# Unsplit tokens from DMAs that add, an earlier pair of gate blocks, and a later due time for the output weights

## The chip, the cores and the metric

The kernel runs on one core of a Trainium2 chip. Its time is the device time of that core in microseconds (us), lower is better. One core has five engines, each with an instruction stream of its own that is executed in order: TensorE (PE, matmuls, with its weight loads shown as PEld), VectorE (DVE), ScalarE (ACT), GpSimd (POOL) and SyncE (SP, which here does nothing but issue DMAs). They meet only through semaphores. DMAs move data beside them.

## The reference

One hybrid layer over 16 meta tokens and 512 tokens, model width 1024. The same RMS-normalised input feeds softmax attention of 8 heads and a gated delta recurrence of 8 heads; each is gated, projected, weighed with a sigmoid, added, projected again and added to the input.

```
hn = rms_norm(h, norm_w)
proj = hn @ w_in
aq, ak, av, az, dq, dk, dv, dz, db, da, ga, gd = split(proj)
o_a = rms_norm(diff_attention(q, k, v, lam), attn_norm_w) * (1 - lam_init)
y_a = (o_a * silu(az)) @ w_branch_attn
qkv = silu(causal_depthwise_conv([dq, dk, dv], conv_w))
o_d = rms_norm(gated_delta_chunked(q, k, v, beta, g), dn_norm_w)
y_d = (o_d * silu(dz)) @ w_branch_delta
merged = sigmoid(ga) * y_a + sigmoid(gd) * y_d
out = rms_norm(h + merged @ w_out, final_norm_w)[:, N_META:]
```

## The kernel before

All of it stays on the chip, in float32 accuracy: each factor of a matmul is split into a high part in a 32-bit format that PE reads in one pass and a low part, what is left (tiles that end in `H` and `L`, or `wh` and `wl`), and three products, high by high, high by low and low by high, are added in PSUM (`PASSES`).

The work is a list of weight blocks of 128 columns (`ORDER`, made by `dense_order`). For each of four groups g there are two heads: keys `dk`, values `dv`, queries `dq` and gates `dz` of the delta rule, and `ak`, `av`, `aq`, `az` of attention. A weight block is fetched by SP into one of four `raw` buffers; ACT rounds it to `wh` and DVE forms `wl` (`load_weights`, `split`). Then PE multiplies it with the tokens `hnH`, `hnL`. Where two blocks come as a pair (`ak` with `av`, and `dk`, `dv` from the second group on) the kernel uses a seven-product scheme in place of eight (`pair_of_blocks`), which needs sums of the tokens too, not only the tokens.

Start: the input comes in as four blocks of 128 tokens `xt` and the 16 meta tokens `mt`. `normalise` takes the squares on ACT, the root on POOL (`rs`), the diagonal `dg` on DVE, and PE transposes and scales at once into a PSUM bank. Out of the bank, `part` writes `hnH` on ACT and `hnL` on DVE. Before the change a third reader, `whole` (L563 to L575), copies the unsplit value from the bank on ACT to the four buffers `room0` to `room3`, one for each half of the channels and each half of the tokens (`whole_`). The bank is free for the next block once both the copy and `hnL` are done. From the `room` buffers `token_sums` (L607) makes four differences on DVE, splits each (`sumH` on ACT, `sumL` on DVE) and so the pairs' sums. It waits for all copies and for the event `ap`, which comes at the end of `gates`, the decays of the delta rule. When the sums are done, `room0`, `room2` and `room3` become buffers for the gated outputs and for the gates `dz`, `az`: a gate block cannot leave its PSUM bank earlier.

End: two branch projections `yd` and `ya` in the same seven-product scheme (`pair_products`), in which ACT takes snapshots `sn` of a running PSUM bank, then the output projection, whose weights `wout` come as eight blocks through the same four `raw` buffers.

The instructions of all engines are put in order when the program is built: a planner (`Plan`) plays the work as tasks with ranks, a cost for each instruction (`Engine.time`), a landing time for each DMA (`transfer`, and `late`, which adds to it) and counts of free buffers, and the order in which an engine is reached is the order of its stream. On the chip each stream is then run in that order, and an instruction that waits holds up all behind it on its engine.

Almost every operation is recorded on one line of a helper (L231), so the profile's groups are told apart by their tiles.

Of the kernel before, what the change touches and what calls it, by code (L numbers as in the profile page):

```python
# [10 lines left out]
F32 = mybir.dt.float32  # L11
# [3 lines left out]
ALU = mybir.AluOpType  # L15
# [5 lines left out]
KB = D // P  # L21
# [12 lines left out]
def dense_order():  # L34

    order = []
    for g in range(H // 2):
        k, v, q, z = ([(n, 2 * g), (n, 2 * g + 1)] for n in ("dk", "dv", "dq", "dz"))
        a0, a1 = ([(n, 2 * g + i) for n in ("ak", "av", "aq", "az")] for i in range(2))
        order += k + v + (a0 + q + z[:1] if g else q + z[:1] + a0) + a1 + z[1:]  # L40
    order += [("gd", c) for c in range(KB)] + [("ga", 0)]
    for n in range(KB):
        order += [("ga", n + 1)] * (n < KB - 1) + [(("yd", "ya")[n // 4], 2 * (n % 4) + i) for i in range(2)]
    return order
# [17 lines left out]
HALF = L // 2  # L62
# [6 lines left out]
PE, DVE, ACT, POOL, SP = "PE", "DVE", "ACT", "POOL", "SP"  # L69
# [19 lines left out]
class Plan:  # L89
# [24 lines left out]
    def spawn(self, gen, rank=None):  # L114
        time, src = self.here() if self.task else (0.0, SP)
        self.tasks.append(Task(gen, self.task.rank if rank is None else rank, time, src))

    def done(self, event):
        self.events[event] = self.here()
# [96 lines left out]
class Engine:  # L216
# [18 lines left out]
    def time(self, op, args, kw):  # L235
        if op == "dma_start":
            return {SP: 60, ACT: 700, POOL: 1050}[self.name]
        out = kw["out"] if "out" in kw else args[0]
        ins = [a for a in list(args[1:]) + list(kw.values()) if hasattr(a, "dtype") and hasattr(a, "space")]
        n = int(np.prod(out.shape[1:]))  # L240
        if self.name == PE:
            if op == "transpose":
                return 2 * max(n / 2.4, 53)
            dt = ins[-1].dtype
            if dt == F32:
                small = ins[0].shape[0] <= 64
                return 2 * max(2 * n / 2.4 + 4, 32 if small else 107)
            if dt == F32R:
                return n / 2.4 + (11 if n < 400 else 18) if n >= 256 else max(2 * n / 2.4, 107)
            return n / 2.4 + 57  # L250
        psum = any(a.space == PSUM for a in ins)
        if op == "tensor_reduce":
            n = int(np.prod(ins[-1].shape[1:]))
        scalar = any(hasattr(kw.get(k), "space") for k in ("scalar", "scalar1", "scale", "bias"))
        if self.name == ACT:
            return (51 if op == "copy" and psum else 94) + n / 1.2 + 50 * scalar + 93 * ("accum_out" in kw)
        if self.name == DVE:
            one = op in ("tensor_copy", "tensor_scalar", "tensor_scalar_mul", "tensor_scalar_add", "memset")
# [7 lines left out]
def hybrid_block(ctx: ExitStack, tc: tile.TileContext, x, meta, wblk, wbd, wout, pcol, prow, out):  # L266
    nc = tc.nc
    plan = Plan({**SLOTS, "wo": 0, "th": 0}, BANKS, ALL_BANKS)
# [32 lines left out]
    def give(kind, at=None):  # L301
        plan.give(kind, names_.index(at.tensor.name) if kind in BANKS else 0)
# [9 lines left out]
    def tick(event, n):  # L312
        ticks[event] = ticks.get(event, 0) + 1
        if ticks[event] == n:
            done(event)
        return ticks[event] == n
# [159 lines left out]
    def load_weights(n):  # L476
        yield ("raw",)
        which = plan.task.slot
        raw = raws[which]
        yield SP  # L480
        m = n - len(ORDER)
        S.dma_start(out=raw, in_=wblk[n] if m < 0 else wout[m // 4, :, m % 4 * D:m % 4 * D + D])
        if n in PAIRED or m < 0 and ORDER[n][0] in ("yd", "ya"):
            first.append((raw, which))
            if len(first) == 2:
                spawn(split_pair(n - 1, tuple(first)), 0)
                first.clear()
        else:
            spawn(split(n, raw, which), 0.3 if n < 2 else 0 if m < 0 else 2)
# [34 lines left out]
    def normalise(n):  # L524

        yield f"x{n}"
        w = P if n == 0 else D
        ss, rs, dg = (mk(sp, [P, k], F32, t, 3) for k, t in ((1, "ss"), (1, "rs"), (P, "dg")))
        yield ACT
        A.activation(out=st[:, :w], in_=xt[n], func=AF.Square, accum_out=ss)  # L530

        def weigh():
            yield "nwb"
            yield DVE
            V.tensor_tensor(out=xt[n], in0=xt[n], in1=mt[:, P:2 * P] if n == 0 else nwb, op=ALU.mult)
# [12 lines left out]
        V.tensor_scalar(out=ss, in0=src, scalar1=1.0 / D, scalar2=EPS, op0=ALU.mult, op1=ALU.add)  # L548
        if n == 0:
            give("pdl", pt)  # L550
        yield POOL
        G.tensor_tensor(out=rs, in0=ss, in1=mhalf[:, 0:1], op=ALU.pow)
        yield DVE
        V.tensor_scalar_mul(out=dg, in0=ident, scalar1=rs)
        yield f"xw{n}"

        def part(pt, dst):
            yield ACT
            A.copy(out=hn[0][dst], in_=pt)
            tick(f"hh{n}", 1 if n == 0 else 2)  # L560
            bank_ = f"hn bank {n} {dst[1].start}"

            def whole():  # L563

                t0, t1 = dst[2].start, dst[2].stop
                for c in (0, KB // 2) if n == 0 else (dst[1].start,):
                    for m in range(2):
                        lo, hi = max(t0, HALF * m), min(t1, HALF * m + HALF)
                        if lo < hi:
                            yield ACT  # L570
                            A.copy(out=whole_[2 * (c // 4) + m][:, :, lo - HALF * m:hi - HALF * m],
                                   in_=pt[:, c - dst[1].start:c - dst[1].start + 4, lo - t0:hi - t0])
                if tick(bank_, 2):
                    give("pat", pt)
                tick("whole", 9)  # L575

            spawn(whole(), 0.6)
            yield DVE
            V.tensor_tensor(out=hn[1][dst], in0=pt, in1=hn[0][dst].bitcast(F32), op=ALU.subtract)
            if tick(bank_, 2):  # L580
                give("pat", pt)
            tick(f"hn{n}", 1 if n == 0 else 2)

        for hf in range(1 if n == 0 else 2):
            yield ("pat",)
            yield PE
            pt = bank("pat")
            if n == 0:
                T.matmul(pt[:, 0:P], xt[0], dg, start=True, stop=True)
                pt = pt[:, 0:P].rearrange("p (k t) -> p k t", t=NM)  # L590
                dst = (slice(None), slice(0, KB), slice(0, NM))
            else:
                pt = pt.rearrange("p (k t) -> p k t", t=P)
                for k in range(4):
                    T.matmul(pt[:, k, :], xt[n][:, (4 * hf + k) * P:(4 * hf + k + 1) * P], dg, start=True, stop=True)
                dst = (slice(None), slice(4 * hf, 4 * hf + 4), slice(NM + P * (n - 1), NM + P * n))
            spawn(part(pt, dst))
# [6 lines left out]
    ts_l = [mk(rp, [P, KB // 2, HALF], F32R, f"sumL{n}") for n in range(4)]  # L604
    of_sum = dict(t1=0, t2=3, t3=1, t4=2)

    def token_sums():  # L607
        yield "whole"
        yield "ap"

        def high_low(key):
            n = of_sum[key]
            yield ACT
            A.copy(out=ts_h[n], in_=whole_[n])
            yield DVE
            V.tensor_tensor(out=ts_l[n], in0=whole_[n], in1=ts_h[n].bitcast(F32), op=ALU.subtract)
            done(key)
            if tick("sums", 4):
                for n in range(SLOTS["th"]):
                    plan.give("th", n)  # L620

        for key, (x_, y_) in dict(t1=(1, 0), t3=(3, 1), t2=(3, 0), t4=(2, 3)).items():
            yield DVE
            V.tensor_tensor(out=whole_[of_sum[key]], in0=whole_[x_], in1=whole_[y_], op=ALU.subtract)
            spawn(high_low(key))
# [1579 lines left out]
```

## Time and profile before

| what | value |
|---|---|
| time, median of 3 runs | 765.07 us (760.48 to 768.07) |
| profiled execution | 767.75 us, span 766.0 us |
| granted TensorE clock, mean | 0.989 |
| instructions | 14381 |
| HBM read, written | 67.58 MB, 6.36 MB |

The span is what the trace shows from the first to the last instruction; the profiled execution's own time is 1.75 us longer. Each engine's row gives its busy time and count. A matmul's duration includes its way through the array, so that dense matmuls overlap in the trace: their cost is the distance between two starts. In a row of the timeline stand the start, the duration, the engine, the operation with output and inputs, the count, and, in brackets, the idle time ahead of it and who ended it.

### The profile page before, as it was taken

To read this page: it belongs to the slowest core of one execution; us is meant where nothing else is said; L and a number is where in the kernel's file an instruction comes from. 1 tells how busy PE (TensorE), PEld (TensorE's weight loads), DVE (VectorE), ACT (ScalarE), POOL (GpSimd) and SP (SyncE) were. 2 spreads that over 40 slices of the span, in tenths; PEclk is the share of its full clock that TensorE was granted. 3 is DMA by queue.
4 is the path that set the end of the run, shared out by engine and by line. 5 is a ranking of instruction groups with operands and counts; after the bars stand their busy time and mean duration, and the time that the engine had idled before them with its cause. 6 is when DMAs were issued, how large, how long until landed. Compare 5 with 4: busy or idle time off the path is not lost.

```text
span 766.0 us, 14381 instructions
## 1 busy us (share of the span) xinstructions
PE 740.0 (97%) x5311; PEld 671.6 (88%) x5311; DVE 620.2 (81%) x1427; ACT 500.4 (65%) x1318; POOL 89.6 (12%) x102
## 2 busy tenths in 40 slices
PE   4999999999999999999999999999999999999996
PEld 4998888899999799999889989988888998898775
DVE  6799999699899659989877979975697879797353
ACT  6479576679865848986587977667776446454132
POOL 4134002112000201401020311000100000000001
PEclk9999999999999979999999999999999999999999
DMA  8031423224304103421320441360123442143502
GB/s 320 30 113 32 135 83 70 70 70 149 98 33 145 31 34 119 147 81 42 118 64 22 159 135 33 120 184 30 56 83 116 147 148 91 57 131 111 193 1 110
DMA packets 45430, 74.86 MB, mean 98 GB/s; under 512 B 20728, under 2 KB 25636, under 8 KB 45360
## 3 DMA queue, kind: packets, MB, share of 16 engines
q1 hardware_dynamic: 45360, 73.95, 30.0%
q8 instruction: 41, 0.67, 0.3%
q14 instruction: 29, 0.24, 0.1%
HBM read 67.58 MB, written 6.36 MB: 97 GB/s over the span
## 4 chain that ended last, share of the span: by engine, by line
PE 74%; DVE 10%; ACT 10%; issue 2%; DMA 1%; POOL 1%; SPq 0%; POOLq 0%; DVEq 0%; ACTq 0%
PE bank L231 71%; PE psc L231 3%; ACT wh L231 2%; DVE wl L231 2%; DVE y L231 1%; ACT TM L231 1%; DMA xt<-in_x_dram 1%; POOL km L231 1%; ACT ak L231 1%; ACT e L231 1%; DMA raw<-in_wout_dram 1%; ACT ktd L231 1%; DVE ak L231 1%; DVE ast L231 1%; ACT y L231 1%
## 5 line engine op out<-in xcount | busy, mean ns | idle before, releaser
L231 PE MATMUL bank<-hnH,wh 128*128 128x512 f32 (+4 forms) x664 | 233.6, 355 | 1.6 <-ACT hnH L231 1.3
L231 PE MATMUL bank<-hnL,wh 128*128 128x512 f32 (+4 forms) x664 | 222.0, 337 | 0.0
L231 PE MATMUL bank<-hnH,wl 128*128 128x512 f32 (+4 forms) x664 | 221.7, 337 | 0.0
L231 DVE TENSOR_TENSOR wl<-raw,wh 128x1024 fp32r<-128x1024 f32 (+1 forms) x120 | 134.4, 1121 | 20.2 <-ACT wh L231 19.6
L231 ACT CAST wh<-raw 128x1024 fp32r<-128x1024 f32 (+1 forms) x120 | 116.4, 970 | 48.6 <-PE bank L231 34.5
L231 PEld LDWEIGHTS bank<-hnH,wh 128*128 128x128 f32 x664 | 124.5, 189 | 14.5 <-ACT hnH L231 1.5
L231 PEld LDWEIGHTS bank<-hnH,wl 128*128 128x128 f32 x664 | 124.3, 189 | 14.0
L231 PEld LDWEIGHTS bank<-hnL,wh 128*128 128x128 f32 x664 | 124.5, 189 | 9.5
L231 PE MATMUL bank<-sumH,wh 128*128 128x264 f32 x224 | 68.0, 303 | 0.0
L231 PE MATMUL bank<-sumL,wh 128*128 128x264 f32 x224 | 63.9, 285 | 0.4 <-DVE sumL L231 0.4
L231 PE MATMUL bank<-sumH,wl 128*128 128x264 f32 x224 | 63.8, 285 | 0.0
L231 DVE SCALAR_TENSOR_TENSOR y<-xp,pc,y 128x528 f32<-128x528 f32 (+1 forms) x72 | 54.1, 757 | 0.5 <-ACT y L231 0.5
L231 ACT ACTIVATE e<-psc,ast 128x144 f32<-128x144 f32 (+3 forms) x64 | 34.7, 542 | 18.4 <-DVE ast L231 16.6
L231 PEld LDWEIGHTS bank<-sumL,wh 128*128 128x128 f32 x224 | 42.6, 190 | 0.6 <-DVE sumL L231 0.6
L231 PEld LDWEIGHTS bank<-sumH,wh 128*128 128x128 f32 x224 | 42.7, 190 | 0.2
L231 PEld LDWEIGHTS bank<-sumH,wl 128*128 128x128 f32 x224 | 42.4, 189 | 0.0
L231 PE MATMUL bank<-btH,wh 128*128 128x256 f32 x128 | 36.2, 283 | 2.1 <-ACT sn L231 2.1
L231 PE MATMUL bank<-btH,wl 128*128 128x256 f32 x128 | 36.0, 281 | 0.0
L231 PE MATMUL bank<-btL,wh 128*128 128x256 f32 x128 | 35.9, 281 | 0.0
L231 POOL TENSOR_TENSOR ass<-ass,mhalf 128x4 f32<-128x4 f32 x8 | 10.3, 1288 | 186.8 <-DVE ass L231 175.2
L231 PE MATMUL psc<-ak,aq 128*128 128x264 f32 (+3 forms) x160 | 29.1, 303 | 0.4 <-ACT e L231 0.3
L231 DVE TENSOR_REDUCE ast<-psc 128x1 f32<-128x528 f32 (+3 forms) x40 | 28.5, 714 | 0.5
(370 smaller groups left out, 1738.2 us busy)
## 6 DMA issues: line engine op xcount, KB each, us to landing
raw<-in_wblk_dram SPq DMA_DIRECT2D x96, 512.0 KB, 3.6
raw<-in_wout_dram SPq DMA_DIRECT2D x8, 512.0 KB, 4.9
xt<-in_x_dram SPq DMA_DIRECT2D x4, 512.0 KB, 6.4
TM<-gcd SPq DMA_DIRECT2D x8, 256.0 KB, 5.9
xr<-in_x_dram SPq DMA_DIRECT2D x8, 256.0 KB, 6.0
out_dram<-xr SPq DMA_DIRECT2D x8, 256.0 KB, 2.1
room<-scrm SPq DMA_DIRECT2D x12, 128.0 KB, 3.5
oad<-room SPq DMA_DIRECT2D x6, 256.0 KB, 2.0
```

Of the source, the lines that this page charges most:

```text
L231: return real(*args, **kw)
```

## The change

Three edits.

1. `whole` no longer copies on ACT out of PSUM. It is a task for each of the four `room` buffers: SP issues a DMA that copies `hnH` (528 KB of it) into the buffer, and when that has landed POOL issues two DMAs, each of which adds half of the `hnL` part to it in flight. `token_sums` waits for all four. In `part` a bank is given back once `hnL` is formed.
2. In the first group the order is now `dk`, `dv`, `dq`, both `dz`, then the four blocks of the first attention head and those of the second; the second `dz` block stood behind the heads before. In the other groups nothing moves.
3. The planner is told that blocks of `wout` land 1600 ns later than it reckoned, and that a small float32 matmul costs 40 ns.

```
-        order += k + v + (a0 + q + z[:1] if g else q + z[:1] + a0) + a1 + z[1:]
+        order += k + v + (a0 + q + z[:1] + a1 + z[1:] if g else q + z + a0 + a1)
...
-                return 2 * max(2 * n / 2.4 + 4, 32 if small else 107)
+                return 2 * max(2 * n / 2.4 + 4, 32 if small else 107) if n > 32 or ins[0].shape[0] > 32 else 40
...
         S.dma_start(out=raw, in_=wblk[n] if m < 0 else wout[m // 4, :, m % 4 * D:m % 4 * D + D])
+        if m >= 0:
+            plan.late(1600)
...
             tick(f"hh{n}", 1 if n == 0 else 2)
-            bank_ = f"hn bank {n} {dst[1].start}"
-
-            def whole():
...
-                            A.copy(out=whole_[2 * (c // 4) + m][:, :, lo - HALF * m:hi - HALF * m],
-                                   in_=pt[:, c - dst[1].start:c - dst[1].start + 4, lo - t0:hi - t0])
-                if tick(bank_, 2):
-                    give("pat", pt)
-                tick("whole", 9)
-
-            spawn(whole(), 0.6)
             yield DVE
             V.tensor_tensor(out=hn[1][dst], in0=pt, in1=hn[0][dst].bitcast(F32), op=ALU.subtract)
-            if tick(bank_, 2):
-                give("pat", pt)
+            give("pat", pt)
...
+    def whole(c, m):
+
+        part = slice(None), slice(KB // 2 * c, KB // 2 * c + KB // 2), slice(HALF * m, HALF * m + HALF)
+        for e in range(1 if m == 0 else 2, 4 if m == 0 else 5):
+            yield f"hh{e}"
+        yield "hh0"
+        yield SP
+        S.dma_start(out=whole_[2 * c + m], in_=hn[0][part].bitcast(F32))
+        plan.late(1500)
+        for e in range(1 if m == 0 else 2, 4 if m == 0 else 5):
+            yield f"hn{e}"
+        yield "hn0"
+        low = hn[1][part].bitcast(F32)
+        for k in (0, 2):
+            yield POOL
+            G.dma_start(out=whole_[2 * c + m][:, k:k + 2], in_=low[:, k:k + 2], accum_op=ALU.add)
+        plan.late(5000)
+        done(f"whole {c}{m}")
+
     def token_sums():
-        yield "whole"
+        for c in range(2):
+            for m in range(2):
+                spawn(whole(c, m))
+        for c in range(2):
+            for m in range(2):
+                yield f"whole {c}{m}"
         yield "ap"
```

Three places show what moves in the streams. The first is ACT at the start, where the tokens come out of PSUM (`hnH` and `room` are written from banks, `st` takes squares, `wh` and `wbs` are weights). Before:

```order
L231 CAST hnH<-bank_5_82 128x4x128
L231 CAST wh_21_118<-raw_15_112 128x1024
L231 COPY room_30_129<-bank_4_81 128x4x128
L231 CAST hnH<-bank_6_83 128x8x16
L231 ACTIVATE st_115,ss_196<-xt_125 128x1024
L231 CAST wbs_203<-wbr_126 128x8x16
L231 COPY room_32_131<-bank_5_82 128x4x128
L231 CAST hnH<-bank_3_80 128x4x128
L231 CAST wh_23_120<-raw_16_113 128x1024
L231 COPY room_30_129<-bank_6_83 128x4x16
L231 COPY room_30_129<-bank_3_80 128x4x120
L231 COPY room_32_131<-bank_6_83 128x4x16
```

The same stretch of ACT now:

```order
L231 CAST hnH<-bank_5_82 128x4x128
L231 CAST hnH<-bank_6_83 128x8x16
L231 CAST wh_21_118<-raw_15_112 128x1024
L231 CAST hnH<-bank_3_80 128x4x128
L231 ACTIVATE st_115,ss_196<-xt_125 128x1024
L231 CAST hnH<-bank_4_81 128x4x128
L231 CAST wbs_203<-wbr_126 128x8x16
L231 CAST wh_23_120<-raw_16_113 128x1024
L231 CAST hnH<-bank_5_82 128x4x128
L231 CAST hnH<-bank_6_83 128x4x128
```

All copies to `room` are gone, and the casts to `hnH` move up. On PE in the same place (`dg` with `xt` is a transpose of a token block, `wh`/`wl` with 272 columns a product of the first two weight blocks, `wbs` the gates), before:

```order
L231 MATMUL bank_3_80<-dg_188,xt_123 128x128 x4
L231 MATMUL bank_4_81<-dg_188,xt_123 128x128 x4
L231 MATMUL bank_5_82<-dg_193,xt_124 128x128 x4
L231 MATMUL bank_1_78<-hnH,wh_19_116 128x272 x7
L231 MATMUL bank_6_83<-dg_193,xt_124 128x128 x4
L231 MATMUL bank_3_80<-dg_198,xt_125 128x128 x4
L231 MATMUL bank_5_82<-dg_198,xt_125 128x128 x4
L231 MATMUL bank_1_78<-hnH,wh_19_116 128x272
L231 MATMUL bank_1_78<-hnH,wl_20_117 128x272
L231 MATMUL bank_4_81<-hnH,wbs_203 32x272 x8
```

And now:

```order
L231 MATMUL bank_4_81<-dg_188,xt_123 128x128 x4
L231 MATMUL bank_1_78<-hnH,wh_19_116 128x272 x8
L231 MATMUL bank_1_78<-hnH,wl_20_117 128x272 x3
L231 MATMUL bank_5_82<-dg_193,xt_124 128x128 x4
L231 MATMUL bank_6_83<-dg_193,xt_124 128x128 x4
L231 MATMUL bank_1_78<-hnH,wl_20_117 128x272 x5
L231 MATMUL bank_1_78<-hnL,wh_19_116 128x272 x8
L231 MATMUL psc_175<-hnH,wh_21_118 128x272 x3
L231 MATMUL bank_3_80<-dg_198,xt_125 128x128 x4
L231 MATMUL bank_4_81<-hnH,wbs_203 32x272 x7
L231 MATMUL bank_5_82<-dg_198,xt_125 128x128 x4
```

Ahead of the last transposes stood 7 products; now 27 and 7 of the gates' matmuls stand there. The second place is POOL behind the roots `rs` of the token blocks, ahead of the `ts` constants of the delta rule and of `km`, the first keys of the meta tokens. Before:

```order
L231 TENSOR_TENSOR rs_192<-ss_191,mhalf 128x1
L231 TENSOR_TENSOR rs_197<-ss_196,mhalf 128x1
L231 MEMSET ts_630 99x352
L231 AFFINE_SELECT ts_630<-ts_630 32x352 x3
L231 AFFINE_SELECT ts_630<-ts_630 3x352
L231 COPY km_622<-kT_585 128x16
```

Now:

```order
L231 TENSOR_TENSOR rs_197<-ss_196,mhalf 128x1
L231 DMA room_30_129<-hnL 128x2x264
L231 DMA room_32_131<-hnL 128x2x264
L231 DMA room_31_130<-hnL 128x2x264
L231 DMA room_30_129<-hnL 128x2x264
L231 DMA room_32_131<-hnL 128x2x264
L231 DMA room_33_132<-hnL 128x2x264
L231 DMA room_31_130<-hnL 128x2x264
L231 DMA room_33_132<-hnL 128x2x264
L231 MEMSET ts_675 99x352
```

Eight DMAs stand between them, two for each `room`. The first token difference, on DVE, is `room_30` from `room_31` and `room_30`: it needs four of the eight, the seventh among them. The third place is the end, ACT in the last pair of the second branch (`sn` are snapshots, `hnL_w` and `wh` from `raw` are output weights). Before:

```order
L231 CAST hnL_w<-raw_15_112 128x1024
L231 CAST hnL_w<-raw_14_111 128x1024
L231 COPY sn_8245<-bank_5_82 128x256
L231 CAST wh_19_116<-raw_17_114 128x1024
L231 COPY sn_8270<-bank_5_82 128x256
L231 CAST wh_23_120<-raw_16_113 128x1024
L231 CAST sumH_862_8329<-sumL_676_6141 128x512
```

Now:

```order
L231 CAST hnL_w<-raw_15_112 128x1024
L231 CAST hnL_w<-raw_14_111 128x1024
L231 COPY sn_8245<-bank_2_79 128x256
L231 COPY sn_8268<-bank_2_79 128x256
L231 CAST wh_19_116<-raw_17_114 128x1024
L231 CAST wh_23_120<-raw_16_113 128x1024
L231 CAST sumH_861_8326<-sumL_684_6173 128x512
```

The last snapshot now stands ahead of both output weights.

More of the change, by code (lines that the diff above doesn't have):

```diff
@@ L560, in part @@
             tick(f"hh{n}", 1 if n == 0 else 2)
-            bank_ = f"hn bank {n} {dst[1].start}"
-            def whole():
[L565 to L570, printed above, removed]
-                            A.copy(out=whole_[2 * (c // 4) + m][:, :, lo - HALF * m:hi - HALF * m],
-                                   in_=pt[:, c - dst[1].start:c - dst[1].start + 4, lo - t0:hi - t0])
-                if tick(bank_, 2):
-                    give("pat", pt)
-                tick("whole", 9)
-            spawn(whole(), 0.6)
             yield DVE
             V.tensor_tensor(out=hn[1][dst], in0=pt, in1=hn[0][dst].bitcast(F32), op=ALU.subtract)
-            if tick(bank_, 2):
-                give("pat", pt)
+            give("pat", pt)
             tick(f"hn{n}", 1 if n == 0 else 2)
```

## The prediction

> **What bounds the kernel now.** I read the page first, then the stretches, then single rows. The page's span, its busy times and its chain of waits:
>
> ```profile
> span 766.0 us, 14381 instructions
> PE 740.0 (97%) x5311; PEld 671.6 (88%) x5311; DVE 620.2 (81%) x1427; ACT 500.4 (65%) x1318; POOL 89.6 (12%) x102
> PE 74%; DVE 10%; ACT 10%; issue 2%; DMA 1%; POOL 1%; SPq 0%; POOLq 0%; DVEq 0%; ACTq 0%
> ```
>
> PE is busy in 740.0 of 766.0 us. The change takes no product away from PE, so all it can win is PE's waiting: 26 us in all, a part of it lead-in and last writes. The stretches (start and end, length, then PE, PEld, DVE, ACT, POOL busy, clock, DMA share, GB/s) say where:
>
> ```profile
> 10.00:20.00 10.00, 6.30 (x42) 5.73 (x41) 9.46 (x15) 9.15 (x20) 5.73 (x5) 1.00 0.86 331
> 20.00:30.00 10.00, 9.93 (x83) 9.14 (x82) 7.14 (x27) 4.56 (x11) 2.65 (x4) 1.00 0.16 55
> 40.00:50.00 10.00, 10.00 (x83) 9.66 (x81) 9.60 (x17) 6.62 (x20) 4.55 (x1) 1.00 0.48 153
> 60.00:80.00 20.00, 18.45 (x129) 16.27 (x128) 19.90 (x32) 16.72 (x40) 6.56 (x6) 1.00 0.03 5
> 80.00:100.00 20.00, 19.61 (x122) 17.39 (x123) 18.27 (x40) 11.95 (x24) 0.00 (x0) 1.00 0.41 129
> 100.00:150.00 50.00, 48.73 (x397) 43.14 (x396) 42.27 (x117) 33.13 (x87) 6.84 (x8) 1.00 0.28 80
> 700.00:766.00 66.00, 57.57 (x305) 49.37 (x303) 27.84 (x50) 19.25 (x36) 3.42 (x4) 0.95 0.31 104
> ```
>
> Three places bear on the change. From 10 to 20 PE idles 3.70 us while DVE and ACT are full (9.46, 9.15). From 60 to 100 it idles 1.55 + 0.39 = 1.94 us, with DVE at 38.17 of 40. At the end there is a single long wait, shown below.
>
> **Part 1a, ACT at the start.** The copies that go, and what PE does around them:
>
> ```profile
> L231 ACT COPY room<-bank x12: 192/572/672, 13.5 to 23.9; 128x512 f32<-128x512 f32 x6, 128x64 f32<-128x64 f32 x2, 128x480 f32<-128x480 f32 x2, 128x32 f32<-128x32 f32 x2
> 17.64 0.75 PE L231 MATMUL bank<-hnH,wh 128*128 128x272 f32 x4
> 19.66 0.65 PE L231 MATMUL bank<-hnH,wh 128*128 128x272 f32 x3 [1.27 <-ACT hnH L231]
> 16.33 0.28 DVE L231 TENSOR_SCALAR dg<-ident,rs 128x128 f32<-128x128 f32 x1
> 20.84 0.28 DVE L231 TENSOR_SCALAR dg<-ident,rs 128x128 f32<-128x128 f32 x1
> 17.72 0.69 DVE L231 TENSOR_TENSOR hnL<-bank,hnH 128x512 fp32r<-128x512 f32 x1
> 23.38 1.19 PE L231 MATMUL bank<-hnH,wbs 128*32 128x272 f32 x8
> 29.83 1.17 PE L231 MATMUL psc<-hnH,wh 128*128 128x272 f32 x8
> 30.84 1.17 PE L231 MATMUL psc<-hnH,wl 128*128 128x272 f32 x8
> ```
>
> Twelve copies end, at the median of 572 ns at most 6.9 us of ACT, between 13.5 and 24.6. What that gives PE is less. The transposes hang on `dg` from DVE, which is full there and loses nothing; in the new order one or two `hnL` of 0.69 us stand ahead of the last `dg`, so the last `dg` comes near 22 instead of 20.84, about 1 us later. The gain is that PE has work meanwhile: 27 products instead of 7, and 7 gate matmuls, stand ahead of the last transposes. Eight products take 30.84 - 29.83 = 1.01 us, so 20 are 2.5 us; the gates' seven are about 1.0 (7/8 of 1.19). That is 3.5 us of work moved into 3.70 us of waiting, less 0.7 for the later block (its 1 us, of which a few products that are left cover 0.3). **I take -2.8 us**, between -3.5 and -1.0 (only the 1.27 us wait on `hnH` gone, less a little).
>
> **Part 1b, the DMAs.** Four copies on SP and eight adding DMAs on POOL must be done when DVE reaches the first difference. The rows that bound them (issues with size and time to landing, SP's last weight loads before them and the next one after, two POOL copies of one shape, the differences):
>
> ```profile
> raw<-in_wblk_dram SPq DMA_DIRECT2D x96, 512.0 KB, 3.6
> TM<-gcd SPq DMA_DIRECT2D x8, 256.0 KB, 5.9
> oad<-room SPq DMA_DIRECT2D x6, 256.0 KB, 2.0
> 16.24 3.65 SPq L231 DMA_DIRECT2D raw<-in_wblk_dram  x2
> 38.36 0.33 SPq L231 DMA_DIRECT2D raw<-in_wblk_dram  x1
> 45.45 5.07 POOL L231 COPY km<-kT 128x16 f32<-128x16 f32 x1 [22.65 <-DVE kT L231]
> 67.69 0.20 POOL L231 COPY vm<-y 128x16 f32<-128x16 f32 x1 [3.09 <-DVE y L231]
> L231 DVE TENSOR_TENSOR room<-room,room x4: 1239/1240/1241, 46.3 to 59.8; 128x1056 f32<-128x1056 f32 x4
> 47.45 1.21 DVE L231 TENSOR_TENSOR wl<-raw,wh 128x1024 fp32r<-128x1024 f32 x1
> 48.59 0.69 DVE L231 SCALAR_TENSOR_TENSOR kT<-xp,y 128x528 f32<-128x528 f32 x1
> 45.61 0.75 DVE L231 SCALAR_TENSOR_TENSOR y<-xp,pc,y 128x528 f32<-128x528 f32 x1
> ```
>
> SP issues the last weight load before them at about 19.9 (16.24 + 3.65), and the next was due only at 38.36, so the copies hold up no weight and start near 20.5. The first lands some 3.6 us on, and POOL begins near 24.5. The first difference began at 46.3; in the new order one `wl`, one `kT` and two `y` more stand ahead of it (1.21 + 0.69 + 2 x 0.75 = 3.4), and all is 2.8 earlier: deadline 46.9, so 22.4 us for eight. None of them waits for the add before it, and from 20 to 30 the DMA engines are 16% busy. The nearest row in size that reads a `room` buffer is `oad<-room`, 2.0 us for 256 KB (its target is outside the core's buffers); the adding ones have 264 KB and also read their target. At 2.0 in series they end at 40.5, at 2.8 at 46.9. I take 2.0 to 2.5, hidden: **0 us**. From above stand 5.07 (a POOL copy that takes 0.20 elsewhere, under a full DVE) and 5.9 (256 KB): ends at 65 or 72, 18 or 25 us late. Behind a waiting difference all of DVE is queued, `wl` and the convolution's `y` among it, and PE for these. POOL's `ts` and `km` wait behind the adds too; `km` is needed only after 24 more products than before (3 us).
>
> The Trainium skill, SBUF — State Buffer, section "Who interferes with whom", has DVE hold the port that POOL's descriptor writing needs during single-source copies in a fast mode, while two-input operations block only POOL's reads; its summary advises against such a DMA beneath DVE work. The 5.07 us `km` copy reads and ran beside two-input work, which agrees; DVE's long operations here have two inputs, so by that page the adds pass and the sum stays, while its advice taken by itself is rival (a). The skill's DMA: Bandwidth & Descriptors ("Anatomy of one DMA") gives 2.0 us plus bytes by 436 GB/s, an estimate of 2.6 us each and 45.3 for the end.
>
> **Part 2, the gate block.** The first use of the sums, and the pace of a gate block:
>
> ```profile
> L231 DVE TENSOR_TENSOR sumL<-room,sumH x4: 1234/1238/1239, 72.0 to 82.5; 128x1056 fp32r<-128x1056 f32 x4
> 81.98 0.39 PE L231 MATMUL bank<-sumL,wh 128*128 128x264 f32 x1 [0.39 <-DVE sumL L231]
> 66.69 0.40 PE L231 MATMUL bank<-hnH,wh 128*128 128x512 f32 x1
> 66.92 0.40 PE L231 MATMUL bank<-hnL,wh 128*128 128x512 f32 x1
> ```
>
> The second `dz` block, 24 products at 0.23 = 5.5 us of PE, now runs ahead of the sums. It gives DVE that long, but DVE is also handed more ahead of the last `sumL` (all eight `MT`, the second `AT`), and PE loses the block later among the heads. Of the 1.94 us idle between 60 and 100 I take half: **-1.0 us**, between 0 and -1.9.
>
> **Part 3, the output weights, and the planner's costs.** The wait at the end:
>
> ```profile
> 707.91 0.28 PE L231 MATMUL bank<-btH,wl 128*128 128x256 f32 x1
> 708.95 1.04 ACT L231 CAST wh<-raw 128x1024 fp32r<-128x1024 f32 x1 [2.86 <-DMA raw<-in_wout_dram]
> 709.90 0.36 ACT L231 COPY sn<-bank 128x256 f32<-128x256 f32 x1
> 710.32 0.39 PE L231 MATMUL bank<-btH,wh 128*128 128x256 f32 x1 [2.12 <-ACT sn L231]
> ```
>
> ACT stood 2.86 us for a weight DMA with the snapshot behind it, and PE 2.12 for the snapshot. Now the snapshot goes first: PE ends its product at 708.2, the snapshot takes 0.36 with about 0.06 on each side (710.26 to 710.32), so PE goes on at about 708.7 instead of 710.32: **-1.6 us**, between -2.1 and -1.0. Next late is the same weight cast, needed only by the second half of the output. The other planner cost shuffles streams everywhere; no row prices it. PE's visible waiting from 100 to 150 is 1.27 us; I take 0, with three such stretches, 4 us, either way.
>
> **Sum.** -2.8 + 0 - 1.0 - 1.6 = -5.4 us. The profiled execution took 767.75 us (span 766.0), so it would be 762.35; it lies 2.7 above the median of 765.07, and on that basis the forecast is **759.7 us**.
>
> **Rivals.** (a) *The adds are late.* For it: the `km` copy and 5.9 us. Against it: 2.0 us for 256 KB. The gain is eaten at a completion 5.4 us past the deadline, 3.5 us for each add; slower by over 1% needs 13 us late, 4.5 each. At 5.07, 18 us late, the time is 765.07 - 5.4 + 18 = 778; at 3.5 it is 765. Chance of the first 0.10, of the second 0.12. (b) *DVE takes the start's gain back*: from 60 to 100 it is full, and PE gets to the sums no sooner. Only the tail is left: 765.07 - 1.6 = 763.5, 0.17. (c) *The shuffle helps*: 4 us more than forecast, 755.7, from heads and recurrence with a better order; the visible waiting from 100 to 150 allows little, but PEld's 43.14 of 50 more; 0.18. (d) *The snapshot still waits* for something else on ACT: 761.3, inside the forecast. The forecast itself has 0.43, (d) within it. That the edits do not do what they say can be left out: the order shows every copy gone and the snapshot moved.
>
> **Numbers.** About 1% (757.4 to 772.7) is what a measurement here can tell from no change; the three runs before span 760.48 to 768.07, and the clock row of 0.95 from 700 to 766 alone is 3.3 us (5% of 66) that another execution may spend elsewhere or not at all. Faster by over 1%: (c) 0.18 and a third of the forecast's 0.43, 0.33 in all. Slower by over 1%: 0.10. Within: 0.57. The range takes in half of (c) and the milder half of (a): 753.5 to 768.5.
>
> **What would show it.** Right: PE busy above 8.5 us of 10 to 20; the last `dg` near 22; the first `room` difference on DVE without a wait on a DMA, between 46 and 49; no wait of PE on `sn` over 0.8 us near the end. Wrong: a wait of DVE on the POOL queue, eight POOL issues that take over 3 us each, or PE idle that reappears between 60 and 150.

## The result and the profile after

| what | before | after |
|---|---|---|
| time, median of six runs | 762.88 us (760.48 to 768.95) | 772.60 us (770.84 to 773.04) |
| profiled execution | 767.75 us, span 766.0 us | 770.84 us, span 769.1 us |
| granted TensorE clock, mean | 0.989 | 0.986 |

The ratio is 1.0108, 95% interval 1.0059 to 1.0156: the change makes the kernel slower by about 1%. The forecast was 759.7 us, and 772.60 lies above its range.

The page of the changed kernel, here its span and busy times, looks almost like that of before; PE is even busy 2.8 us less:

```profile
span 769.1 us, 14403 instructions
PE 737.2 (96%) x5311; PEld 670.6 (87%) x5311; DVE 617.6 (80%) x1427; ACT 494.8 (64%) x1306; POOL 89.2 (12%) x110
```

The stretches say where the time went (start and end, length, then PE, PEld, DVE, ACT, POOL busy, clock, DMA share, GB/s):

```profile
10.00:20.00 10.00, 7.75 (x48) 7.12 (x48) 9.56 (x15) 7.05 (x14) 4.61 (x3) 0.89 0.90 334
20.00:30.00 10.00, 10.00 (x81) 9.61 (x80) 5.36 (x24) 2.80 (x7) 1.87 (x2) 0.94 0.88 260
50.00:60.00 10.00, 5.63 (x49) 5.42 (x47) 0.01 (x1) 3.41 (x15) 1.20 (x2) 0.94 0.53 105
60.00:80.00 20.00, 11.45 (x81) 11.25 (x82) 16.18 (x32) 11.73 (x34) 12.96 (x12) 0.69 0.25 66
```

From 50 to 80 PE is idle 4.37 + 8.55 = 12.92 us. In the kernel before it idled 1.55 us from 60 to 80 and not at all from 50 to 60:

```profile
50.00:60.00 10.00, 10.00 (x88) 9.83 (x87) 8.75 (x26) 8.94 (x30) 4.40 (x4) 1.00 0.27 101
```

In the changed kernel DVE does nothing at all from 50 to 60. Three views of this place, POOL's timeline, the waiting rows of DVE, ACT and PE, and the issues with their time to landing, give the cause:

```profile
25.80 1.39 POOL L231 DMA_DIRECT2D room<-hnL  x1 [5.32 <-DMA room<-hnH]
31.08 1.23 POOL L231 DMA_DIRECT2D room<-hnL  x1 [3.89 <-issue]
35.17 1.19 POOL L231 DMA_DIRECT2D room<-hnL  x1 [2.86 <-DVE pp L231]
39.25 1.21 POOL L231 DMA_DIRECT2D room<-hnL  x1 [2.90 <-issue]
44.34 1.18 POOL L231 DMA_DIRECT2D room<-hnL  x1 [3.88 <-issue]
48.81 1.20 POOL L231 DMA_DIRECT2D room<-hnL  x1 [3.29 <-DVE y L231]
55.94 1.19 POOL L231 DMA_DIRECT2D room<-hnL  x1 [5.93 <-issue]
60.02 1.21 POOL L231 DMA_DIRECT2D room<-hnL  x1 [2.88 <-issue]
66.01 2.23 POOL L231 COPY km<-kT 128x16 f32<-128x16 f32 x2
59.99 1.26 DVE L231 TENSOR_TENSOR room<-room,room 128x1056 f32<-128x1056 f32 x1 [10.15 <-DMA room<-hnL]
68.27 0.23 ACT L231 ACTIVATE sqm<-km 128x32 f32<-128x32 f32 x1 [14.09 <-POOL km L231]
68.56 0.27 PE L231 MATMUL bank<-ones,sqm 128*32 128x1 f32 x2 [12.93 <-ACT sqm L231]
room<-hnL POOLq DMA_DIRECT2D x8, 264.0 KB, 4.0
```

An add occupies POOL for 1.2 us and lands 4.0 us after its issue (median). The next is issued only then: between two issues lie (60.02 - 25.80) / 7 = 4.89 us. DVE's first difference needs the seventh add, issued at 55.94 and landed at 59.99, and waits 10.15 us for it. POOL's `ts` and `km` stand behind the eighth, ACT's `sqm` waits for `km`, and PE 12.93 us for `sqm`. The idle time between two adds is put down to "issue" or to a result of DVE, so these rows name no cause. The DMA packets in the same trace say more: each of the seven later adds is issued 0.58 to 0.70 us after the last packet of the add before it.

Two things are better than before, the start and the end. PE is busy 7.75 us of 10 to 20 in place of 6.30, and its wait on the snapshot (2.12 us before) is 0.46:

```profile
715.15 0.39 PE L231 MATMUL bank<-btH,wh 128*128 128x256 f32 x1 [0.46 <-ACT sn L231]
```

### The profile page after: what moved, and what is told of

Its sections match the earlier page's. It is cut to its first block, busy times and chain, and to the rows that moved or that the text cites. A ratio compares the mean times of both kernels' runs of the same rounds, so it can differ in the third digit from the quotient of the medians.

```text
span 769.1 us, 14403 instructions
## 1 busy us (share of the span) xinstructions
PE 737.2 (96%) x5311; PEld 670.6 (87%) x5311; DVE 617.6 (80%) x1427; ACT 494.8 (64%) x1306; POOL 89.2 (12%) x110
## 3 DMA queue, kind: packets, MB, share of 16 engines
q0 software_dynamic: 2176, 2.16, 1.9%
## 4 chain that ended last, share of the span: by engine, by line
PE 78%; DVE 12%; issue 3%; POOL 2%; DMA 1%; ACT 1%; SPq 1%; POOLq 0%; DVEq 0%; ACTq 0%
PE bank L231 75%; PE psc L231 3%; DVE wl L231 2%; DVE y L231 2%; DVE ts L231 1%; DVE tmps L231 1%; DMA xt<-in_x_dram 1%; DVE aq L231 1%; DVE ast L231 1%; POOL ts L231 1%; DVE qT L231 1%; SPq L231 1%; DVE room L231 1%; DVE raw L231 0%; POOL room L231 0%
## 5 line engine op out<-in xcount | busy, mean ns | idle before, releaser
L231 PE MATMUL bank<-sumH,wl 128*128 128x264 f32 x224 | 63.6, 284 | 0.0
L231 PE MATMUL bank<-sumL,wh 128*128 128x264 f32 x224 | 63.6, 284 | 0.0
L231 ACT ACTIVATE e<-psc,ast 128x144 f32<-128x144 f32 (+3 forms) x64 | 34.7, 544 | 16.2 <-DVE ast L231 16.1
L231 ACT CAST wh<-st 128x1024 fp32r<-128x1024 f32 x22 | 23.1, 1051 | 14.9 <-PE bank L231 10.7
```

The source lines that it names most:

```text
L231: return real(*args, **kw)
```

## Experiments

All times below are medians, with the ratio to the kernel before on the same chip and its 95% interval. The first group asks why the adds go one at a time. The program reserves 1024 bytes of each state-buffer partition for the descriptors of DMAs that POOL issues (`dynamic_dma_scratch_size`). **Theory 1**: the space holds one add, and the next waits for it to be free. **Theory 2**: each add is slow in itself. The state buffer is full, so a larger space has to be paid for with two shorter rings of buffers.

**e1: more space for descriptors**

```
- dynamic_dma_scratch_size=1024       + dynamic_dma_scratch_size=1856
- u = mk(dp, [P, P], F32, "u", 4)     + u = mk(dp, [P, P], F32, "u", 3)
- ... [P, P], F32, "S", 6)            + ... [P, P], F32, "S", 5)
```

> The changed kernel with 1856 bytes of descriptor space in each partition for POOL's DMAs in place of 1024; two rings of state buffers in the recurrence are one buffer shorter (u 4 to 3, S 6 to 5) to make room. Theory 1 (POOL can issue an adding DMA only when the descriptor space of the one before it is free again, so that the eight go one at a time, 4.9 us apart): the first issues stand 1.2 to 2 us apart, the eight end near 45 to 48 us instead of 64, DVE's first room difference waits under 1 us for a DMA, the 13 us gap of PE goes, and the time is 756 to 760. Theory 2 (each add is slow in itself, from its reading of the target or from traffic of DVE and the weight loads): the spacing stays 4 to 5 us, the gap stays, 770 to 773.

Measured 756.58 us, ratio 0.9907 (0.9875 to 0.9939): faster than both kernels. The planner knows nothing of the space and, as both traces show, writes the same instructions in the same order on every engine, so these are the changed kernel's streams with other waits. POOL's timeline and two stretches:

```profile
26.08 1.38 POOL L231 DMA_DIRECT2D room<-hnL  x1 [5.48 <-DMA room<-hnH]
28.82 1.20 POOL L231 DMA_DIRECT2D room<-hnL  x1 [1.37 <-DMA room<-hnH]
30.51 1.18 POOL L231 DMA_DIRECT2D room<-hnL  x1 [0.49 <-DVE z L231]
32.89 2.49 POOL L231 DMA_DIRECT2D room<-hnL  x2 [1.20 <-issue]
35.62 1.19 POOL L231 DMA_DIRECT2D room<-hnL  x1 [0.24 <-issue]
37.07 1.18 POOL L231 DMA_DIRECT2D room<-hnL  x1 [0.26 <-issue]
40.64 1.20 POOL L231 DMA_DIRECT2D room<-hnL  x1 [2.39 <-issue]
50.00:60.00 10.00, 10.00 (x87) 9.82 (x86) 9.95 (x24) 9.91 (x33) 2.83 (x4) 1.00 0.31 94
60.00:80.00 20.00, 19.89 (x124) 17.33 (x123) 19.87 (x35) 17.07 (x47) 1.91 (x3) 1.00 0.18 49
```

The issues are 2.08 us apart on average, though each add now takes longer (6.2 us at the median, up to three in flight). PE's gap is gone, and so is every wait of DVE for an add. The other DMAs, DVE's work and the weights are the same as in the changed kernel, so theory 2 falls. The packets agree with theory 1: in the changed kernel no earlier add is unfinished at any issue, in e1 at most two are. In e1 the packets of the adds follow one another without a pause from 28.75 to 46.64 us, so there the moving of the data sets the pace.

**e9, control: the shorter buffers alone** (`u` 3, `S` 5, space 1024)

> Control of the run with 1856 bytes: the changed kernel with the two shorter rings of buffers (u 3, S 5) and the descriptor space left at 1024. If the space alone made the gain: 770 to 773, adds 4 to 5 us apart, the gap of 13 us in place. If the shorter buffers had a part in it: below 768.

Measured 772.75 us, ratio 1.0127 (1.0091 to 1.0164): the shorter buffers give nothing. The last add was issued at 62.40, 5.21 us to an add, and the groups of PE's waits (total, times, longest) have an even longer one. PE came to it 1.6 us earlier in this execution (the first product of `dq` is at 50.61, in the changed kernel at 52.24), and `sqm` came 2.4 us later (70.94 against 68.56):

```profile
62.40 1.21 POOL L231 DMA_DIRECT2D room<-hnL  x1 [2.90 <-issue]
PE bank L231 <- ACT sqm L231: 17.3, 2, 16.9
```

**e16: a space between the two** (1536 bytes, `u` 3)

> The changed kernel with 1536 bytes of descriptor space (u 3). An add seems to need more than half of 1024 bytes, so that a second does not fit. If an add needs 513 to 768 bytes, two fit in 1536: issues in pairs, mean spacing 2.2 to 3, the last near 46 to 48, the gap of PE under 3 us, 757 to 761. If the space is given back only when an add has landed and one needs over 768 bytes: no better than 1024, 770 to 773.

Measured 758.71 us, 0.9941 (0.9913 to 0.9968). POOL's timeline and DVE's waits, the first and the last issue and the pair between them:

```profile
26.03 1.38 POOL L231 DMA_DIRECT2D room<-hnL  x1 [5.60 <-DMA room<-hnH]
...
32.98 2.55 POOL L231 DMA_DIRECT2D room<-hnL  x2 [2.83 <-DVE pp L231]
...
46.20 1.20 POOL L231 DMA_DIRECT2D room<-hnL  x1 [1.20 <-issue]
49.55 1.26 DVE L231 TENSOR_TENSOR room<-room,room 128x1056 f32<-128x1056 f32 x1 [1.26 <-DMA room<-hnL]
```

They are 2.88 us apart, between the 4.89 of 1024 bytes and the 2.08 of 1856. DVE waits for adds twice, 3.8 us in all, where it waited 12.3 with 1024 bytes and not at all with 1856; PE idles 2.72 us from 50 to 60. By the packets at most one earlier add is unfinished at an issue. So 1024 bytes hold one add, 1536 two and 1856 three. If the space is given out in proportion to their number, an add needs more than 512 and at most 618 bytes.

**e2: sixteen adds of half the size** (space 1024)

```
- for k in (0, 2): ... [:, k:k + 2]
+ for k in range(4): ... [:, k:k + 1]
```

> The changed kernel with sixteen adds of 132 KB in place of eight of 264 KB, the descriptor space as it is. Theory 1 (space): three or so are in flight at a time, issues 1 to 1.5 us apart, all landed near 46 to 50, the gap of PE is mostly gone, 757 to 762. Theory 2, limited by bytes: as before, all landed near 64, 770 to 773. Theory 2, limited by a fixed time of each in series: sixteen by 4 us from 25 on, landed near 89, about 795.

The adds behaved as theory 1 says: three issues in 2.65 us at 31.79, the last at 47.50, at most two earlier adds unfinished at an issue, and no gap of PE at 55. The time was 783.88 us all the same, ratio 1.0259 (1.0207 to 1.0312). Eight more issues had made the planner write a new order, and PE now waited elsewhere (5.1 us for `sumL`, 4.5 for `vT`, 3.8 for `vm`).

This kernel's output is wrong. The delta rule fetches a small table (`room<-scrm`) into `room1`, and the task that fetches it waits for the table alone, not for the token sum that is still read from there. In the changed kernel the planner happens to put that read first; in e2 and in e12 below it puts the fetch first, so the sum is wrong, and DVE also stands 3.00 us for the fetch ahead of its second `sumL` (3.08 in e12). The times of the adds' issues do not depend on it; the total times of these two kernels carry little weight. That a new order costs so much is the second question.

**e4: the adds left out** (only SP's copies stay)

```
- for k in (0, 2): G.dma_start(out=whole_[...], in_=low[...], accum_op=ALU.add)
- plan.late(5000)
```

> The changed kernel without its eight adding DMAs: the four SP copies stay, so the pairs' sums are made of the high parts alone and the low parts are left out of them. If the adds carry the whole loss: the gap at 55 to 68 us goes. With a start's gain of 0.5 us (as the changed kernel's trace suggests) 759 to 760, with the forecast's 2.8 us 757. If the SP copies themselves are late or take DMA time from the weights, PE waits on weights between 25 and 60 and the time stays above 763.

Measured 754.59 us, 0.9877 (0.9817 to 0.9937). That is below what was expected. The token sums lack the low parts, but the order of all engines is that of the changed kernel without the eight adds. PE is busy in 74.87 of the 75 us from 25 to 100, so the copies on SP hold up no weight that PE needs there. Against e1 the median is 756.6 - 754.6 = 2.0 us less. The adds themselves are little of it: in the two traces the same product of PE is only 0.1 us apart at 207 us, long after the last add, and 1.5 us at the end. Where the rest comes from was not found.

**e12: the planner told how long an issue holds POOL** (space 1024)

```
- return {SP: 60, ACT: 700, POOL: 1050}[self.name]
+ return {SP: 60, ACT: 700, POOL: 4000}[self.name]
```

> The changed kernel at 1024 bytes, with the planner told that a DMA issue holds POOL for 4000 ns in place of 1050 (the trace showed 4.9 us between issues). The adds stay as slow as they are. If the loss is one of order (POOL's ts and km, and DVE's other work, stuck behind the adds): the planner puts km and ts between or ahead of the last adds and other work ahead of the room differences, the gap of 13 us falls under 4 and the time is 757 to 763. If the sums are needed by PE at that point whatever the order: the gap stays above 8 us, 766 to 773.

Measured 775.85 us, 1.0169 (1.0145 to 1.0193). The planner moved `km` ahead of the last two adds and PE's wait on `sqm` fell to 4.8 us, but 6.6 us for `sumL` came in its place. The output is wrong as in e2, and half of the new wait comes from that: DVE stands 3.08 us for the fetch into `room1`.

```profile
93.43 3.60 DVE L231 TENSOR_TENSOR sumL<-room,sumH 128x1056 fp32r<-128x1056 f32 x3 [3.08 <-DMA room<-scrm]
```

The time lies above both expected ranges, and the run does not decide between them. It shows only that PE's wait on `sqm` gets shorter when `km` is ahead of the last adds.

The second question is the planner's. Each part alone:

```
e8:  part 1 only (order, price, due time as before; space 1024)
e3:  parts 2 and 3 only (ACT copies as before)
e5:  order of the first group only
e6:  price of small products only
e7:  plan.late(1600) for wout only
```

> Part 1 alone, with the descriptor space of 1024 bytes: copies on SP and adds on POOL in place of the ACT copies, order and prices as before. The adds one at a time, 4.9 us apart, end near 64 again. With one dz block less to run ahead of the sums (5.5 us of PE), PE's gap is 13 + 5 = 18 us instead of 13, and the time is 762.8 - 0.5 - 2 + 18 = 778, between 772 and 784. If the changed kernel's loss came from the order or the prices and not from the adds: 758 to 764.

Measured 779.24 us, 1.021 (1.0126 to 1.0294), as expected: PE waits 15.6 us on `sqm` and 2.7 on `sumL`.

> Parts 2 and 3 alone (order of the first group, the output weights planned 1600 ns later, the price of small products), with the ACT copies as before. If the adds alone carry the loss: 762.9 - 1.0 - 1.6 = 760.3, between 758 and 763. If the new order or the planner's prices shuffle work for the worse: 766 to 771.

Measured 783.56 us, 1.0258 (1.0204 to 1.0311): without any add, slower than the changed kernel. Both expectations missed. There is no single wait; PE's rows and POOL's show several, among them:

```profile
56.35 8.90 POOL L231 TENSOR_TENSOR sc<-sc,phalf 128x4 f32<-128x4 f32 x1
56.00:64.00 8.00, 8.00 (x69) 8.00 (x69) 8.00 (x14) 5.78 (x16) 8.00 (x2) 1.00 0.27 83
69.79 0.28 PE L231 MATMUL bank<-ident,vm 128*32 128x128 f32 x1 [3.16 <-POOL vm L231]
241.46 0.39 PE L231 MATMUL bank<-hnH,wh 128*128 128x264 f32 x1 [3.46 <-DVE vT L231]
300.00:400.00 100.00, 93.70 (x707) 84.50 (x706) 88.36 (x220) 66.79 (x193) 13.12 (x17) 0.97 0.30 91
```

> Part 2 alone: in the first group both dz blocks run ahead of the first heads; everything else as before. If the order of the first group made the 20 us that parts 2 and 3 lost without the DMAs: 775 to 785, with PE waiting between 60 and 80 and again from 200 to 600. If the price of small products made them: 758 to 764. If it takes both: 760 to 768.

Measured 766.87 us, 1.0053 (1.0021 to 1.0084), in the range of "it takes both".

> The new price of the small matrix products alone (40 ns in the planner's clock for at most 32 rows by 32 columns); everything else as before. If the price made the 20 us: 775 to 785, with PE idle from 200 to 600. If the order made them: 759 to 767. If it takes both: 760 to 768.

Measured 769.75 us, 1.0077 (1.0042 to 1.0111), in none of the three ranges.

> The output weights planned 1600 ns later alone; everything else as before. The order up to the last 60 us is that of before, so if the tail's step was read rightly PE's last wait on the snapshot falls from 2.12 to under 0.6 us and the time is 1.6 us less: 761.2 against 762.8. If something else on ACT holds the snapshot: 762.8.

Measured 760.02 us, 0.9951 (0.9908 to 0.9994), 2.4 us by the medians, with an interval from 0.5 to 7.0 us. It is the one edit that stays local: PE's order is that of before, product for product, and DVE's and ACT's differ in nine places near the end.

**e10 and e13: plans that change no work.** The planner's allowance for a signal from DVE, in the kernel before:

```
- HOP = {PE: 200, DVE: 130, ACT: 140, POOL: 90, SP: 0}
+ HOP = {PE: 200, DVE: 131, ACT: 140, POOL: 90, SP: 0}      (and 132)
```

> The kernel before, with one number of the planner's clock changed by 1 ns (what it allows for a signal from DVE: 131 for 130). No operation is added, removed or made longer; the planner writes the instructions in another order from there. If the plan is robust, so that a difference of several us between two of these kernels has a cause of its own: 761 to 765. If any touch of the planner makes a new plan whose time scatters by 10 us, which would carry the losses of the new order and of the new price: outside 759 to 767.

> The kernel before with the planner's allowance for a signal from DVE at 132 ns in place of 130; no work changes. With 131 it took 767.9. If any new plan scatters by several us: again away from the kernel before by 2 us or more, and by another amount than with 131. If 131 had a cause of its own: 762 to 764.5.

Measured 767.86 us, 1.0066 (1.0042 to 1.0091), and 766.99 us, 1.004 (1.0007 to 1.0073). One nanosecond in the planner's arithmetic puts another product in 2714 of PE's 5311 places, the first of them the 123rd, and costs about as much as the new order of part 2 did. The second run adds little to the first, since the two orders are nearly the same (PE's differ in 53 places).

**e11, e14, e15 and e1: order and price with the space in place** (1856 bytes, later weights in all; e11 has both old, e14 the new order, e15 the new price)

| | price old | price new |
|---|---|---|
| order old | 761.55 (0.9986; 0.9957 to 1.0015) | 774.42 (1.0148; 1.009 to 1.0207) |
| order new | 776.08 (1.016; 1.0089 to 1.023) | 756.58 (0.9907; 0.9875 to 0.9939) |

> Part 1 with 1856 bytes of descriptor space (buffers u 3, S 5) and the output weights planned later; order of the first group and price of small products as in the kernel before. Part 1 alone at 1024 bytes took 779.2; if all of its loss is the serial adds, 18 us of gap go and the later weights bring 2.4: about 759, between 756 and 762. If the order of the first group is needed as cover for the adds (5.5 us of products), PE still waits some 3 to 5 us for the sums: 761 to 765. If the plan scatters: anything from 755 to 775, with waits spread over the heads.

> The changed kernel with 1856 bytes of space (u 3, S 5) and the old price of small products: order new, price old. If the new price is what makes the plan good with the DMAs in: 760 to 765. If the order does it, as cover of 5.5 us of products ahead of the sums: 756 to 758, with PE's wait for sumL near 77 us under 0.5 us. If the plans scatter: 756 to 775, with the waits spread over the heads.

> The same with the order of the first group old and the price new. If the order is needed: PE waits 2 to 3 us for sumL near 77 us, as with order and price both old (761.6), and the time is 759 to 764. If the price alone brings it: 756 to 758. If the plans scatter: 756 to 775, with the waits spread over the heads.

Each edit alone loses 13 to 15 us against neither, and both together gain 5. No mechanism that the prediction has for the order or the price does that. The kernel with both old (e11) has PE's order of e8, product for product, and takes 17.7 us less (761.55 against 779.24), with more space, the two shorter rings and the later weights as the only differences: a second pair, beside the changed kernel and e1, for what the adds cost one at a time. The one local effect that was expected is there: with the old order PE waits for `sumL`, 2.67 us with the old price and 2.08 with the new (e15), and with the new order (e14 and e1) it does not. With both old:

```profile
50.85 0.28 PE L231 MATMUL bank<-hnH,wh 128*128 128x258 f32 x1
80.48 0.39 PE L231 MATMUL bank<-sumL,wh 128*128 128x264 f32 x1 [2.67 <-DVE sumL L231]
138.42 1.09 PE L231 MATMUL bank<-TM,MT 32*32 32x32 f32 x32
```

**e17 and e18: the kernel of e1 with another price**

```
- ... else 40        + ... else 38        (and 42)
```

> The fastest kernel (all parts, 1856 bytes, u 3, S 5) with small products priced at 38 ns in place of 40. If the edits carry the gain: 755.5 to 758.5. If it belongs to one plan among many: off 756.6 by 3 us or more, as far as 776, with waits on kT, vT and ao spread over the heads from 200 to 520.

> The same with 42 ns. If the edits carry the gain: 755.5 to 758.5. If it belongs to one plan among many: off 756.6 by 3 us or more, and by another amount than with 38.

Measured 772.41 us, 1.0113 (1.0069 to 1.0158), and 756.91 us, 0.991 (0.9882 to 0.9938). So e18 lies where "the edits carry the gain" put it, and e17 where "one plan among many" did. The two kernels have the same DMAs, the same order of the weight blocks and the same arithmetic. Compared with e1, e18 has another product in 1277 of PE's places, the first after 1863, and e17 in 2869, the first after 976. From 300 to 500 PE idles 3.69 + 4.56 = 8.25 us with 38, first, and 1.57 with 42, second:

```profile
300.00:400.00 100.00, 96.31 (x730) 86.76 (x729) 84.40 (x224) 67.86 (x196) 13.22 (x15) 0.98 0.26 78
400.00:500.00 100.00, 95.44 (x706) 89.11 (x705) 88.65 (x221) 75.70 (x212) 14.54 (x15) 1.00 0.31 100
```

```profile
300.00:400.00 100.00, 99.20 (x761) 90.04 (x760) 86.51 (x218) 73.96 (x210) 12.02 (x15) 1.00 0.30 91
400.00:500.00 100.00, 99.23 (x732) 92.87 (x731) 90.50 (x239) 78.66 (x239) 12.19 (x14) 1.00 0.36 113
```

Over the whole span PE idles 28.7 us with 38 and 20.2 with 42, and it is busy 742.5 and 736.1 us for the same products. Two spells at half clock with 38, 3.4 us each at 366 and 499 us, are about half of the longer busy time; the rest was not followed.

So a new order, a plan, is much like a draw. Without the adds, the five that changed the order early on (e3, e5, e6, and e10 and e13, which are nearly one) lie 2 to 20 us above the kernel before; with the adds and 1856 bytes, the six lie between 756.6 and 776.1. Why one plan is good and its neighbour is not stays open. The traces show that a part of the losses is many waits of 1 to 4 us, on `vT`, `kT`, `ao`, `vm` and `pmT` among others, where PE comes to a product before its input is there.

## Why the prediction was wrong

**The step that failed is 1b**, and in it the sentence "None of them waits for the add before it". Nothing in the program makes an add wait, but the space for descriptors does. The price was wrong too: 2.0 us for 256 KB came from `oad<-room`, a plain copy on another queue, and 2.5 was taken as the upper value; an add alone took 4.0 to land. Either error without the other would have been harmless: with several in flight the adds are hidden, though each takes longer to land (e1), and one at a time at 2.0 to 2.5 us each they would have ended before the deadline by the prediction's own sum. The arithmetic of rival (a) was sound. At 4.89 us each from 24.5 on it gives an end at 63.6, 17 us past the deadline of 46.9; PE waited 12.9. With e1 as the same streams without that wait, the serial adds cost 772.6 - 756.6 = 16.0 us. In the two profiled executions the same product of PE is 1.5 us later than in e1 at 50 us, from a lower clock at the start, and 16.2 us later at 73 us; in between lie the wait of 12.93 and 1.7 us from PE running at half clock after it. Of the signs that were named for being wrong, DVE's wait on the adds and PE's idle time came; POOL's issues stayed at 1.2 us each, since the time lay between them. The right rival had a chance of 0.22 in all, and 0.10 for over 1%. The rows gave a warning that was read as an end of the range only: two far prices, 5.07 and 5.9.

**The rule on the shared port agrees with the traces as far as they go.** By the Trainium skill, SBUF — State Buffer, "Who interferes with whom", two-input operations of DVE do not hold up the writing of descriptors (the page calls this inferred). The adds held POOL 1.18 to 1.39 us each, with DVE idle (the changed kernel, 1.19 at 55.94) or in a two-input operation (e1, 1.19 at 35.62):

```profile
34.82 1.23 DVE L231 TENSOR_TENSOR wl<-raw,wh 128x1024 fp32r<-128x1024 f32 x1
```

The same section has such operations block POOL's reads. The 8.90 us `sc` in e3 lies beside a DVE that is busy in all of the 8.00 us from 56 to 64, and `sc` takes 1.0 to 2.2 us in the changed kernel, which agrees; but in e1 two of them, at 54.61, took 2.19 us together with DVE busy in 9.95 of 10 us, so what makes one long was not shown. The estimate by the Trainium skill, DMA: Bandwidth & Descriptors ("Anatomy of one DMA"), 2.6 us, was short: 4.0 measured.

**1a, the start, was right.** The first product of `dq` shows what PE gains:

```profile
52.93 0.28 PE L231 MATMUL bank<-hnH,wh 128*128 128x258 f32 x1
```

```profile
50.74 0.28 PE L231 MATMUL bank<-hnH,wh 128*128 128x258 f32 x1
```

The first is the kernel before, the second e1, each behind the same 319 products: 2.2 us, where 2.8 was forecast, between 1.0 and 3.5. In the profiled execution of the changed kernel it is 52.24, since the clock was 0.89 and 0.94 from 10 to 30. The last `dg` came at 21.32 in e1 (near 22 was said), PE was busy 8.76 us of 10 to 20 (over 8.5). But with the adds late, an earlier start only makes the wait longer (e9).

**Rival (b) is there in the old order.** In e11 PE is 2.1 us ahead at the first `dq`, waits 2.67 for `sumL`, and at the `TM` block stands at 138.42, against 138.33 before: DVE has taken the gain back. With the new order there is no such wait: e1 idles 0.11 us from 60 to 100.

**2, the gate block.** In e1 PE idles 0.11 us where it idled 1.94: 1.8, at the far end of the bounds (0 to 1.9, taken 1.0). The mechanism was right and the size low, in that plan. The edit alone cost 4.5 us, because it also drew a new plan.

**3, the tail, was right**: 2.12 to 0.46 is 1.66, where 1.6 was forecast; alone it measured 2.4.

**The planner's costs, "0, with 4 us either way", were badly bounded.** With 1a, 2 and 3 as measured, 2.2 + 1.8 + 1.7 = 5.7 us are explained of the 6.6 that e1 gained, so in the plan on record this term was about -1. That was luck: with 38 ns it would have been about +13. The six plans with 1856 bytes lie 20 us apart, so the range would have had to reach as far upwards. The forecast of 5.4 us without the adds' wait thus comes close to e1, but the same argument would have missed by 13 to 23 us for e3, e14, e15 and e17.

## What to carry to other kernels

Price a row of DMAs by how many may be in flight, not only by how long one takes: look up what limits their number (here the space for descriptors). A row of issues with a pause before each, for which the profile names no cause, can be a sign of such a limit; compare each issue with the last packet of the DMA before it. Where a planner orders the program, first time a change of it that adds no work: a difference within that scatter can't be put down to the edit. A new order can also change the result, where two tasks share a buffer and only the old order kept them apart. A step that was hidden stays hidden only until its last part, so compare the end of the whole row with the deadline, and ask what stands behind it in the same stream.

## What the hardware showed

- The 264 KB adds from state buffer to state buffer took 4.0 us from issue to landing one at a time (median) and 6.2 with up to three in flight, but followed one another every 2.08 us then, in place of 4.89.
- An add took more than 512 and at most 618 bytes of descriptor space in each partition, as worked out from how many were in flight with three sizes, if they share the space in proportion. By the Trainium skill, DMA: Bandwidth & Descriptors ("Terms"), a descriptor has 16 bytes; the 2176 packets of eight adds are 17 for each of 16 engines. That gives an estimate of 272 bytes for an add, and three would fit in 1024. The runs show one; what takes the rest was not seen.
- PE's clock fell to half in the gap and came back late. In the changed kernel PE's last product before the gap begins at 55.35 and the first after it at 68.56; the stretches of 2 us have the clock at 0.71 from 58, 0.50 from 60 to 72 and 0.88 from 72, so some 4 us of work after the wait ran at half speed:

```profile
58.00:60.00 2.00, 0.00 (x0) 0.00 (x0) 0.01 (x1) 0.00 (x0) 0.00 (x0) 0.71 0.73 109
60.00:62.00 2.00, 0.00 (x0) 0.00 (x0) 1.93 (x2) 0.00 (x0) 1.91 (x3) 0.50 0.11 16
...
70.00:72.00 2.00, 2.00 (x11) 2.00 (x11) 1.62 (x6) 2.00 (x8) 2.00 (x2) 0.50 0.45 174
72.00:74.00 2.00, 2.00 (x17) 2.00 (x17) 1.44 (x4) 2.00 (x4) 2.00 (x3) 0.88 0.00 0
```

- One small POOL operation (128 x 4) took from 1.0 to 8.90 us; the longest (e3) ran beside a full DVE, but others beside a full DVE did not take long (e1).
